# A two-layer decoder trunk in split fp32r: a mean subtracted by VectorE, single PSUM banks in four places, block moves on two queues, one more group by seven products

## The chip, the cores and the metric

The kernel runs on one core of one Trainium2 chip. The metric is the device time of one launch in microseconds, the median of three runs: 2025.73 us for the kernel before (2024.69 to 2026.8). All times below are microseconds unless marked otherwise.

## The reference, cut to what matters

One sequence of 256 tokens, 2048 features, two layers, all in float32. Layer 0 mixes by causal pooling over windows of 2, 4, 8 and 16 tokens, layer 1 by dilated causal attention with 16 heads of 128, whose K and V are computed from the stream behind layer 0. Each mixer and each FFN ends in a residual with DeepNorm and a LayerNorm:

```python
for i in range(DEPTH):
    mix = pool_mixer(h, ...) if i < N_A_LAYERS else dilated_attention(h, k_shared, v_shared, ...)
    h = layer_norm(DEEPNORM_ALPHA * h + mix, ln1_g[i], ln1_b[i])
    u = h @ w_up                      # 2048 -> 2 * 5504
    c = causal depthwise conv of u, width 3, with bias
    gate, val = split(c)
    ff = (silu(gate) * val) @ w_down  # 5504 -> 2048
    h = layer_norm(DEEPNORM_ALPHA * h + ff, ln2_g[i], ln2_b[i])
```

## The kernel before, in words

**Units.** The work is a list of weight units, each a block of 512 rows by up to 512 columns of one matrix. `run_units` takes them in order. For each unit SP loads the raw block (L89), ScalarE rounds it to fp32r as `wh` (L99, a cast), VectorE takes the rest `wl = raw - wh` (L100), and TensorE multiplies both halves with the two halves of the activations, `xc`. Three small products thus stand for one float32 product (L180 and L181, or L183 to L185). Units are loaded and split several units ahead of their use. Work that follows a unit is put off by `later(n, fn)`, which runs `fn` n units on; `before[i]` runs just ahead of unit i. This order of the code is the order of each engine's queue. Tile pools add the waits: a tile that is taken again waits for the last reader of the old one.

**Seven products.** Most blocks of the down projections and of V are multiplied by seven half-size products instead of eight (a form of Strassen's scheme). Such a block is split by `split_sums` into a unit "a" and a unit "b" (L113 and L119 on ScalarE; L114, L120, L121, L122 and L124 on VectorE, which also forms sums of parts of the weights). On TensorE a block by seven has 42 matmuls of 256 columns (L244 to L246), a plain one 24 of 512 (L255 to L257). `sevens[q]` in `ffn` says for which of the four column groups c of the down projection the row quarter q goes by seven. `down(2)` of layer 0 multiplies the quarters 7 and 6; its four column groups are woven between the halves of `up(9)` and `up(10)`.

**LayerNorm by features.** H[0] to H[3] hold the stream as [128, 4, 256] quarters of the features, XC the split copies. `add_last` adds the last projection to H, one column group c at a time. Behind c = 0, `shift` takes an estimate of the mean, and subtracts it from the quarters: H[0] by VectorE (L394) and, in the FFN LayerNorm of layer 0 (`first` false), H[1] to H[3] by three accumulating DMAs on GpSimd's queue (L409). Then each group c adds its products to H[c] (L338, L340), sums and squares are folded into S and Q (L364, L367, L370), and `chain` sums them over partitions on TensorE (L429, L430), from which the norm is built (L434 to L444, L305). Meanwhile TensorE runs a first projection of the unnormalised quarters `xp` (L183 to L185).

**Moves.** Before and after the down projection, the stream is turned between features and tokens: `to_tokens` (all four quarters in both layers) and `to_features` (four column groups in layer 0) transpose 32 by 32 blocks on VectorE (L807, L835) and `moves` carries the blocks across partitions by 16 DMAs per quarter, issued by SP in three parts over three units (L825). `to_tokens` uses one `hb` tile for all quarters of a layer. GpSimd's queue holds the accumulating DMAs of the down projection (L287), half of the moves of the attention (L1101) and the three of L409.

**PSUM.** The pool `psp` has four tiles of two banks. `pair` takes one, `bank` takes one and uses only its first half. A tile's dependences are tracked for the whole pair: at the start `x_quad` writes both halves of a quarter into one pair (L548) and then copies (L553, ScalarE), subtracts (L554, VectorE), copies, subtracts. `outputs` of the attention puts two heads into one pair (L1114, L1115) and evacuates them (L1119, L1120). `finish1` at the very end puts three results into two pairs (L940, L947, L952, L955).

Of the kernel before, what the change touches and what calls it, by code (L numbers as in the profile page):

```python
# [9 lines left out]
F32 = mybir.dt.float32  # L10
# [7 lines left out]
T = 256  # L18
# [14 lines left out]
def trunk(ctx: ExitStack, tc: tile.TileContext, x, pool_w_in, pool_w_grp, pool_scale, pool_w_out,  # L33
# [348 lines left out]
    def shift(s, first, lay, which):  # L382
# [10 lines left out]
        def one():  # L393
            V.tensor_tensor(H[0], H[0], cb, OP.add)  # L394
            if first:
                pre(1)
            stats(0)
# [15 lines left out]
        if not first:  # L413
            for q in (1, 2, 3):
                less(q)
# [120 lines left out]
    def x_quad(q, halves=(0, 1)):  # L536
        xin = XIN
        if halves[0] == 0:
            H[q] = hp.tile([P, 4, T], F32, name="h", tag="h")
            XC[q] = quad_tile("xc")  # L540
        if halves[0] == 0:
            ST["xT"] = pair("xT")
        both = ST["xT"]
        for half in halves:
            for kk in range(2):
                for t in range(2):
                    k = 2 * half + kk
                    PE.transpose(both[:, half, kk * T + t * P:kk * T + t * P + P], xin[q, t][:, k * P:(k + 1) * P],  # L548
                                 ident)
        for half in halves:  # L550
            pv2 = both[:, half, :].rearrange("p (k t) -> p k t", k=2)
            s = slice(2 * half, 2 * half + 2)
            A.copy(XC[q][:, s, 0, :T], pv2)  # L553
            V.tensor_tensor(XC[q][:, s, 1, :T], pv2, XC[q][:, s, 0, :T].bitcast(F32), OP.subtract)  # L554
        if halves[-1] == 1:
            before.setdefault(min(q + 1, 3), []).append(
                lambda: A.copy(H[q], both.rearrange("p b (k t) -> p (b k) t", k=2)))
# [26 lines left out]
    def ffn(lay):  # L584
# [9 lines left out]
        else:  # L594
            sevens[7] = (0, 1)
# [220 lines left out]
    def moves(fr, to):  # L816
# [3 lines left out]
        def part(i, n):  # L820
            if i == 0:
                dst.append(to().rearrange("p (k a j) -> p a k j", k=8, a=4))
            for ab in range(i, i + n):
                a, b = ab // 4, ab % 4
                nc.sync.dma_start(dst[0][32 * b:32 * b + 32, a], fr[32 * a:32 * a + 32, b])  # L825
# [38 lines left out]
    def tm_post(lay, n, c):  # L864
# [68 lines left out]
        def finish1():  # L933
# [4 lines left out]
            ps = [p[:, i, :] for p in (pair("gb"), pair("gb")) for i in range(2)]  # L938
# [166 lines left out]
    def outputs(hq, ms):  # L1105
# [3 lines left out]
        both = pair("o")  # L1109
        for m in ms:  # L1110
            hd = slice(m * P, (m + 1) * P)
            ps = both[:, m % 2, :]
# [3 lines left out]
        o = oq[hq][:, ms[0]:ms[0] + 2]  # L1116
        for at in (slice(0, 1), slice(1, 2)) if hq == 3 else (slice(0, 2),):
            hi = o[:, at, 0, :T]
            A.copy(hi, both[:, at, :T])  # L1119
            V.tensor_tensor(o[:, at, 1, :T], both[:, at, :T], hi.bitcast(F32), OP.subtract)  # L1120
# [157 lines left out]
```

## Time and profile before

| what | value |
|---|---|
| median of 3 runs | 2025.73 us (2024.69 to 2026.8) |
| the profiled execution, its own time | 2024.98 us |
| span of its trace, first to last instruction | 2023.2 us |
| mean granted TensorE clock | 0.999 |
| TensorE matmul (PE) busy | 2011.6 us, 99% |
| VectorE (DVE) busy | 1728.5 us, 85% |
| ScalarE (ACT) busy | 1269.2 us, 63% |
| GpSimd (POOL) busy | 94.3 us, 5% |

The profiled execution's own time is 1.78 us above the span, since it has what lies around the first and the last instruction, and 0.75 us under the median. Rows of the trace have the start in us from the span's start, the duration, the engine, the line and operation, the tiles, how often, and in brackets the idle time ahead of it with what ended it. Matmuls are pipelined, so a row's duration overlaps the next: what a matmul costs is the distance between starts.

### The profile page before, as it was taken

How to read it: one execution, taken by the hardware profiler on the slowest of the kernel's cores; microseconds unless marked ns; L12 is line 12 of the kernel's file. 1: busy time of each engine (PE TensorE's matmuls, PEld its weight loads, DVE VectorE, ACT ScalarE, POOL GpSimd, SP SyncE). 2: the span in 40 equal slices, each digit the busy share in tenths (PEclk: the TensorE clock that was granted, in tenths of full speed). 3: DMA queues.
4: the chain of work that ended last, by engine and by line, in shares of the span. 5: the costliest groups of instructions: out<-in, count | busy, mean ns of one | idle time of the engine just before them, and what ended most of it. 6: DMA issues, size and time to landing. Idle time of an engine off the chain costs nothing.

```text
span 2023.2 us, 31428 instructions
## 1 busy us (share of the span) xinstructions
PE 2011.6 (99%) x12742; PEld 1813.7 (90%) x12742; DVE 1728.5 (85%) x1822; ACT 1269.2 (63%) x1546; POOL 94.3 (5%) x154
## 2 busy tenths in 40 slices
PE   9999999999999999999999999999999999999999
PEld 8898988999899988888898988998899989989987
DVE  6868887999899999779796878787899899989898
ACT  5454686766766676656554444477767677667672
POOL 2000000000000000000000021000000000000000
PEclk9999999999999999999999999999999999999999
DMA  8565576676666767885565656557666757666765
GB/s 256 192 211 188 164 216 191 180 221 222 197 198 205 233 190 219 236 226 187 177 207 165 199 175 207 188 175 221 167 215 203 227 179 227 193 222 189 211 220 173
DMA packets 271825, 408.30 MB, mean 202 GB/s; under 512 B 74446, under 2 KB 86116, under 8 KB 271424
## 3 DMA queue, kind: packets, MB, share of 16 engines
q1 hardware_dynamic: 259488, 388.93, 59.1%
q0 software_dynamic: 11760, 16.70, 5.5%
q8 instruction: 100, 1.64, 0.3%
q10 hardware_dynamic: 432, 0.66, 0.1%
q14 instruction: 45, 0.37, 0.1%
HBM read 380.01 MB, written 2.10 MB: 189 GB/s over the span
## 4 chain that ended last, share of the span: by engine, by line
PE 98%; DVE 1%; DMA 0%; issue 0%; ACT 0%; SPq 0%; DVEq 0%
PE acc L180 44%; PE acc L181 22%; PE s L246 3%; PE s L244 3%; PE s L245 3%; PE acc L185 3%; PE t L246 2%; PE t L244 2%; PE t L245 2%; PE acc L184 2%; PE acc L183 2%; PE t L255 2%; PE t L257 2%; PE t L256 2%; PE s L1064 0%; PE o L1114 0%
## 5 line engine op out<-in xcount | busy, mean ns | idle before, releaser
L180 PE MATMUL acc<-xc,wh 128*128 128x512 f32 x3264 | 1151.8, 396 | 0.0
L181 PE MATMUL acc<-xc,wl 128*128 128x256 f32 x3264 | 916.0, 281 | 0.0
L100 DVE TENSOR_TENSOR wl<-raw,wh 128x2048 fp32r<-128x2048 f32 (+2 forms) x305 | 657.1, 2163 | 174.9 <-ACT wh L99 170.3
L180 PEld LDWEIGHTS acc<-xc,wh 128*128 128x128 f32 x3264 | 616.0, 189 | 143.3
L99 ACT CAST wh<-raw 128x2048 fp32r<-128x2048 f32 (+2 forms) x305 | 548.7, 1805 | 170.1 <-PE acc L180 70.4
L181 PEld LDWEIGHTS acc<-xc,wl 128*128 128x128 f32 x3264 | 615.4, 189 | 0.1
L113 ACT CAST wh<-raw 128x1024 fp32r<-128x1024 f32 x142 | 148.4, 1052 | 194.5 <-DVE raw L122 175.3
L114 DVE TENSOR_TENSOR wl<-raw,wh 128x1024 fp32r<-128x1024 f32 x142 | 169.4, 1221 | 11.2 <-ACT wh L113 11.2
L121 DVE TENSOR_TENSOR wl<-raw,wh 128x1536 fp32r<-128x1536 f32 x71 | 124.5, 1754 | 6.7 <-ACT wh L119 5.7
L119 ACT CAST wh<-raw 128x1536 fp32r<-128x1536 f32 x71 | 104.9, 1477 | 35.4 <-PE acc L180 28.2
L287 POOL DMA_DIRECT2D ht<-w x48 | 41.3, 1014 | 1446.7 <-DVE ht L877 722.1
L246 PE MATMUL t<-wh,g 128*128 128x256 f32 x376 | 105.7, 281 | 0.0
L244 PE MATMUL t<-wh,g 128*128 128x256 f32 x376 | 105.6, 281 | 0.0
L245 PE MATMUL t<-wl,g 128*128 128x256 f32 x376 | 105.4, 280 | 0.0
L620 ACT ACTIVATE c<-u,cv 128x256 f32<-128x256 f32 x172 | 89.5, 592 | 23.1 <-DVE f L682 16.6
L246 PE MATMUL s<-wh,xs 128*128 128x256 f32 x344 | 96.2, 280 | 0.0
L244 PE MATMUL s<-wh,xs 128*128 128x256 f32 x344 | 96.1, 279 | 0.0
L245 PE MATMUL s<-wl,xs 128*128 128x256 f32 x344 | 96.0, 279 | 0.0
L124 DVE TENSOR_TENSOR raw<-raw 128x1024 f32<-128x1024 f32 x71 | 87.0, 1225 | 2.4
L625 ACT ACTIVATE a<-u,cv 128x256 f32<-128x256 f32 x172 | 73.4, 499 | 11.9 <-DVE g L692 11.9
L611 ACT COPY u<-acc 128x512 f32<-128x512 f32 x84 | 46.9, 573 | 47.4 <-PE acc L181 47.1
L625 ACT ACTIVATE u<-u,cv 128x256 f32<-128x256 f32 x172 | 73.4, 499 | 0.0
(337 smaller groups left out, 3445.2 us busy)
## 6 DMA issues: line engine op xcount, KB each, us to landing
raw<-in_ffn_w_up_dram SPq DMA_DIRECT2D x160, 1024.0 KB, 5.2
raw<-in_ffn_w_down_dram SPq DMA_DIRECT2D x80, 1024.0 KB, 5.2
raw<-in_pool_w_out_dram SPq DMA_DIRECT2D x16, 1024.0 KB, 5.0
raw<-in_shared_w_k_dram SPq DMA_DIRECT2D x16, 1024.0 KB, 5.1
raw<-in_attn_w_q_dram SPq DMA_DIRECT2D x16, 1024.0 KB, 5.1
raw<-in_shared_w_v_dram SPq DMA_DIRECT2D x16, 1024.0 KB, 5.2
raw<-in_attn_w_o_dram SPq DMA_DIRECT2D x16, 1024.0 KB, 5.4
ht<-w POOLq DMA_DIRECT2D x50, 256.0 KB, 5.3
```

What stands on the lines that cost most here:

```text
L99: A.copy(wh[i][:, s], r[:, s])
L100: V.tensor_tensor(wl[i][:, s], r[:, s], wh[i][:, s].bitcast(F32), OP.subtract)
L113: A.copy(h[:, :, n], r[:, :, n])
L114: V.tensor_tensor(l[:, :, n], r[:, :, n], h[:, :, n].bitcast(F32), OP.subtract)
L119: A.copy(hs, rs)
L121: V.tensor_tensor(ls, rs, hs.bitcast(F32), OP.subtract)
L180: PE.matmul(ps[m].ap, h[:, k, c], q[:, k, :, :T], start=st, stop=False)
L181: PE.matmul(ps[m][:, :T], l[:, k, c], q[:, k, 0, :T], start=False, stop=sp)
L244: PE.matmul(to, xh, h[:, k, n], start=opens and kk == 0, stop=False)
L245: PE.matmul(to, xh, l[:, k, n], start=False, stop=False)
L246: PE.matmul(to, xl, h[:, k, n], start=False, stop=ends and kk == 1)
L625: A.activation(to[:, m, :], u[:, m, i:i + T], AF.Copy, scale=cv[:, i, j:j + 1])
```

## The change

It has four parts. Lines of the kernel after are given as "after L…".

1. In `shift`, H[1] of layer 0's FFN LayerNorm gets its mean subtracted by VectorE (after L398), right behind H[0]. Only H[2] and H[3] are left to GpSimd's accumulating DMAs.
2. Single PSUM tiles in four places: `x_quad` uses a `bank` for each half, and H is copied in two halves and a unit earlier (after L553); `finish1` uses three banks; `outputs` for the heads 2 and 3 of the last head quarter uses a bank for each head and evacuates each as soon as it is issued; the heads 0 and 1 of that quarter are evacuated together.
3. `moves` issues every second of its 16 DMAs from GpSimd's queue (after L822).
4. `sevens[7]` of layer 0 holds the column group 2 too.

```diff
         def one():
             V.tensor_tensor(H[0], H[0], cb, OP.add)
             if first:
                 pre(1)
+            else:
+                V.tensor_tensor(H[1], H[1], cb, OP.add)
             stats(0)
...
         if not first:
-            for q in (1, 2, 3):
+            for q in (2, 3):
                 less(q)
...
-        if halves[0] == 0:
-            ST["xT"] = pair("xT")
-        both = ST["xT"]
         for half in halves:
+            ps = bank("xT")
             for kk in range(2):
                 for t in range(2):
                     k = 2 * half + kk
-                    PE.transpose(both[:, half, kk * T + t * P:kk * T + t * P + P], xin[q, t][:, k * P:(k + 1) * P],
-                                 ident)
-        for half in halves:
-            pv2 = both[:, half, :].rearrange("p (k t) -> p k t", k=2)
+                    PE.transpose(ps[:, kk * T + t * P:kk * T + t * P + P], xin[q, t][:, k * P:(k + 1) * P], ident)
+            pv2 = ps.rearrange("p (k t) -> p k t", k=2)
             s = slice(2 * half, 2 * half + 2)
             A.copy(XC[q][:, s, 0, :T], pv2)
             V.tensor_tensor(XC[q][:, s, 1, :T], pv2, XC[q][:, s, 0, :T].bitcast(F32), OP.subtract)
-        if halves[-1] == 1:
-            before.setdefault(min(q + 1, 3), []).append(
-                lambda: A.copy(H[q], both.rearrange("p b (k t) -> p (b k) t", k=2)))
+            before.setdefault(q, []).append(lambda s=s, pv2=pv2: A.copy(H[q][:, s, :], pv2))
...
-            sevens[7] = (0, 1)
+            sevens[7] = (0, 1, 2)
...
-                nc.sync.dma_start(dst[0][32 * b:32 * b + 32, a], fr[32 * a:32 * a + 32, b])
+                by = nc.sync if ab % 2 == 0 else nc.gpsimd
+                by.dma_start(dst[0][32 * b:32 * b + 32, a], fr[32 * a:32 * a + 32, b])
...
-            ps = [p[:, i, :] for p in (pair("gb"), pair("gb")) for i in range(2)]
+            ps = [bank("gb") for cc in range(3)]
...
-        both = pair("o")
+        last = hq == 3 and ms[0] == 2
+        both = None if last else pair("o")
         for m in ms:
             hd = slice(m * P, (m + 1) * P)
-            ps = both[:, m % 2, :]
+            ps = bank("o") if last else both[:, m % 2, :]
             t = pT.pop((hq, m))
             PE.matmul(ps[:, :T], vt[:, 0, hd], t[:, :T], start=True, stop=False)
             PE.matmul(ps[:, P:T], vt[:, 1, hd], t[:, T:], start=False, stop=True)
-        o = oq[hq][:, ms[0]:ms[0] + 2]
-        for at in (slice(0, 1), slice(1, 2)) if hq == 3 else (slice(0, 2),):
-            hi = o[:, at, 0, :T]
-            A.copy(hi, both[:, at, :T])
-            V.tensor_tensor(o[:, at, 1, :T], both[:, at, :T], hi.bitcast(F32), OP.subtract)
+            if last:
+                hi = oq[hq][:, m, 0, :T]
+                A.copy(hi, ps[:, :T])
+                V.tensor_tensor(oq[hq][:, m, 1, :T], ps[:, :T], hi.bitcast(F32), OP.subtract)
+        if not last:
+            o = oq[hq][:, ms[0]:ms[0] + 2]
+            A.copy(o[:, :, 0, :T], both[:, :, :T])
+            V.tensor_tensor(o[:, :, 1, :T], both[:, :, :T], o[:, :, 0, :T].bitcast(F32), OP.subtract)
```

VectorE's queue in the FFN LayerNorm of layer 0, from the split ahead of `one` to the first addition of column group 1 (`cs` is the negative mean, `fold` and `sq` are folding space, `acc` the group's PSUM); before:

```order
L100 TENSOR_TENSOR wl_8478<-raw_8392,wh_8477 128x1536
L394 TENSOR_TENSOR h<-h,cs 128x1024
L364 TENSOR_TENSOR fold<-h 128x512
L367 TENSOR_TENSOR S<-fold 128x256
L364 TENSOR_TENSOR fold<-sq 128x512
L367 TENSOR_TENSOR Q<-fold 128x256
L338 TENSOR_TENSOR h<-h,acc 128x512
```

and after:

```order
L100 TENSOR_TENSOR wl_8512<-raw_8427,wh_8511 128x1536
L394 TENSOR_TENSOR h<-h,cs 128x1024
L398 TENSOR_TENSOR h<-h,cs 128x1024
L364 TENSOR_TENSOR fold<-h 128x512
L367 TENSOR_TENSOR S<-fold 128x256
L364 TENSOR_TENSOR fold<-sq 128x512
L367 TENSOR_TENSOR Q<-fold 128x256
L338 TENSOR_TENSOR h<-h,acc 128x512
```

One instruction of 128x1024 comes in between the subtraction of H[0] and the folds; on GpSimd's queue one of the three accumulates goes.

VectorE's queue around the splits of `down(2)`'s column group 2 in layer 0, from the last plain split ahead of it (L849 to L880 and their like are evacuations of the group before, `hb<-ht` is the transpose of `to_features`); before:

```order
L100 TENSOR_TENSOR wl_7557<-raw_7485,wh_7556 128x2048
L100 TENSOR_TENSOR wl_7595<-raw_7514,wh_7594 128x2048
L120 TENSOR_TENSOR raw_7554<-raw_7554 128x2x256
L121 TENSOR_TENSOR wl_7633<-raw_7554,wh_7632 128x2x768
L122 TENSOR_TENSOR raw_7554<-raw_7554 128x2x256
L124 TENSOR_TENSOR raw_7554<-raw_7554 128x4x256
L835 STREAM_TRANSPOSE hb<-ht 128x2x4x128
L114 TENSOR_TENSOR wl_7676<-raw_7554,wh_7675 128x4x256 x2
```

and after:

```order
L100 TENSOR_TENSOR wl_7563<-raw_7493,wh_7562 128x2048
L120 TENSOR_TENSOR raw_7522<-raw_7522 128x2x256
L121 TENSOR_TENSOR wl_7603<-raw_7522,wh_7602 128x2x768
L122 TENSOR_TENSOR raw_7522<-raw_7522 128x2x256
L124 TENSOR_TENSOR raw_7522<-raw_7522 128x4x256
L114 TENSOR_TENSOR wl_7642<-raw_7522,wh_7641 128x4x256 x2
L832 STREAM_TRANSPOSE hb<-ht 128x2x4x128
L120 TENSOR_TENSOR raw_7600<-raw_7600 128x2x256
L121 TENSOR_TENSOR wl_7684<-raw_7600,wh_7683 128x2x768
L122 TENSOR_TENSOR raw_7600<-raw_7600 128x2x256
L124 TENSOR_TENSOR raw_7600<-raw_7600 128x4x256
```

One L100 of 2048 elements has become L120, L121, L122, L124 and two L114; what follows stands a unit later.

ScalarE's queue at the start, from the first quarter of x to the third (`xc<-xT` are the copies out of PSUM, `wh` the casts of the first weights); before:

```order
L553 CAST xc<-xT 128x2x256
L99 CAST wh_173<-raw_93 128x512
L553 CAST xc<-xT 128x2x256
L99 CAST wh_173<-raw_93 128x512 x3
L553 CAST xc<-xT 128x2x256 x2
L99 CAST wh_256<-raw_115 128x512 x4
L557 COPY h<-xT 128x1024
L553 CAST xc<-xT 128x2x256 x2
```

and after:

```order
L551 CAST xc<-xT 128x2x256
L99 CAST wh_173<-raw_93 128x512
L551 CAST xc<-xT 128x2x256
L99 CAST wh_173<-raw_93 128x512 x3
L553 COPY h<-xT 128x512 x2
L551 CAST xc<-xT 128x2x256 x2
L99 CAST wh_260<-raw_115 128x512 x4
L553 COPY h<-xT 128x512 x2
```

The copies of H stand a unit earlier, ahead of the next quarter's casts, and in two halves. On GpSimd's queue there are 96 moves more (after L822), and on SP's 96 fewer: in each part of six or five, SP now has three or two.

## Prediction

> **What bounds the kernel now.** I read the share of busy time first, then which engine TensorE's waits name, then the timelines of the places that the change touches. The engine row, and the waits of TensorE (line waited at, releaser, us in total, times, longest):
>
> ```profile
> PE 2011.6 (99%) x12742; PEld 1813.7 (90%) x12742; DVE 1728.5 (85%) x1822; ACT 1269.2 (63%) x1546; POOL 94.3 (5%) x154
> PE acc L429 <- DVE S L370: 2.6, 1, 2.6
> PE acc L185 <- DVE wl L100: 0.9, 3, 0.3
> PE acc L430 <- DVE Q L370: 0.8, 1, 0.8
> PE acc L180 <- DVE o L1120: 0.5, 2, 0.2
> ```
>
> TensorE is busy for 2011.6 of the span of 2023.2 us. So only two things can shorten the run much: fewer matmul starts, or the few places where TensorE stands. The waits name them: 3.4 us at the sums of one LayerNorm (L429, L430), 0.9 at the start (L185), 0.5 behind the attention's last outputs (L180). VectorE, at 85%, is next, and wherever the change gives it work I ask what has it idle there. I sum against the profiled execution's own time, 2024.98, which is 0.75 under the median of 2025.73.
>
> **A. H[1]'s mean by VectorE.** VectorE around the subtraction, the window up to the sums, then the end of the chain (start, duration, engine, line, tiles, count, idle ahead and its releaser; the window's row has length, then busy us of PE, PEld, DVE, ACT, POOL):
>
> ```profile
> 893.01 1.22 DVE L394 TENSOR_TENSOR h<-h,cs 128x1024 f32<-128x1024 f32 x1
> ...
> 896.32 0.43 DVE L367 TENSOR_TENSOR Q<-fold 128x256 f32<-128x256 f32 x1
> 901.48 0.69 DVE L338 TENSOR_TENSOR h<-h,acc 128x512 f32<-128x512 f32 x1 [4.73 <-DMA h<-cs]
> ...
> 901.48:931.00 29.52, 29.18 (x225) 27.98 (x223) 29.11 (x40) 12.72 (x18) 0.00 (x0) 1.00 0.70 206
> ...
> 932.78 0.43 DVE L370 TENSOR_TENSOR S<-S,fold 128x256 f32<-128x256 f32 x1
> ...
> 934.30 0.43 DVE L370 TENSOR_TENSOR Q<-Q,fold 128x256 f32<-128x256 f32 x1
> ```
>
> VectorE stands 4.73 us for the accumulate into H[1], and from there works 29.11 of 29.52 us up to the sums that TensorE waits for: the stall is carried whole to S and Q. With one more instruction like L394 (1.22) VectorE goes on at 896.75 + 1.25 = 898.0 instead of 901.48, 3.5 earlier. S is then ready at 933.21 − 3.5 = 929.7, Q at 934.73 − 3.5 = 931.2. TensorE there:
>
> ```profile
> 924.73 0.28 PE L183 MATMUL acc<-xp,wh 128*128 128x258 f32 x1
> ...
> 930.38 0.28 PE L185 MATMUL acc<-xp,wl 128*128 128x258 f32 x1
> ...
> 935.45 0.78 PE L183 MATMUL acc<-xp,wh 128*128 128x258 f32 x1
> ...
> 938.31 0.28 PE L183 MATMUL acc<-xp,wh 128*128 128x258 f32 x1
> ```
>
> The last column group's products end where the first row begins, 924.73, and its addition now wanted at 930.28 − 3.5 = 926.8, so these results are no limit. From 924.73 to 930.38 there are 47 steps, 0.120 each. The next projection starts at 935.45. The same place in layer 0's first LayerNorm has no stall:
>
> ```profile
> 224.03 0.28 PE L185 MATMUL acc<-xp,wl 128*128 128x258 f32 x1
> ...
> 224.82 0.47 PE L183 MATMUL acc<-xp,wh 128*128 128x258 f32 x1
> ```
>
> There the sums take 0.79 from start to start, here 5.07: 4.28 lost. Behind the stall the matmuls are slow: 12 steps from 935.45 to 938.31 take 2.86 instead of 1.44, another 1.42. That makes 5.7 in all. Q comes 0.3 late for a chain without a stall (L430 would start at about 930.9), which leaves 5.4. Next behind it stands the split of the normalised quarter:
>
> ```profile
> 951.29 1.22 DVE L305 TENSOR_TENSOR xc<-h,xc 128x1024 fp32r<-128x1024 f32 x1
> ...
> 954.18 0.39 PE L180 MATMUL acc<-xc,wh 128*128 128x512 f32 x1
> ```
>
> It is done at 952.51, 1.67 ahead of its first use. VectorE gains 3.5 and TensorE 5.4, so 1.9 are asked of these 1.67: 0.2 lost, and as much again may be lost at the later quarters. I take **−5.0**, with bounds from −5.7 to −1.5 (where ScalarE's casts, which stand between VectorE's instructions, allow only a part of the 3.5).
>
> **B. Seven products.** TensorE over the plain block, the seven-product block behind it and the next unit; VectorE's instructions of a seven-product split; and two idle stretches of VectorE there:
>
> ```profile
> 807.75 0.40 PE L255 MATMUL t<-wh,g 128*128 128x512 f32 x1
> ...
> 813.32 0.28 PE L244 MATMUL s<-wh,g 128*128 128x256 f32 x1
> ...
> 818.27 0.39 PE L180 MATMUL acc<-xc,wh 128*128 128x512 f32 x1
> ```
>
> ```profile
> 815.08 1.76 DVE L100 TENSOR_TENSOR wl<-raw,wh 128x1536 fp32r<-128x1536 f32 x1 [3.38 <-DMA h<-hb]
> ...
> 828.72 0.68 DVE L120 TENSOR_TENSOR raw<-raw 128x512 f32<-128x512 f32 x1
> ...
> 832.98 1.24 DVE L835 STREAM_TRANSPOSE hb<-ht 128x1024 f32<-128x1024 f32 x1
> 834.14 2.31 DVE L114 TENSOR_TENSOR wl<-raw,wh 128x1024 fp32r<-128x1024 f32 x2
> ```
>
> The plain block takes 5.57, one by seven 4.95: **−0.6**. VectorE pays 4.26 (L120 to L124, from 828.72 to 832.98) + 2.31 (two L114) for one plain split of 2048 elements, about 2.3 by scaling L100's 1.76 for 1536: 4.3 more. Its cover is idle time: VectorE stands 3.38 us right there before L100, and the stretch after has more:
>
> ```profile
> 850.00:882.00 32.00, 32.00 (x184) 27.95 (x183) 21.77 (x19) 17.78 (x19) 1.72 (x2) 1.00 0.84 237
> ```
>
> (10.2 us without work in 32). So I cost it at nothing. If the cover is gone, because the 3.38 is taken by other splits that come due at once, up to 4.3 arrive at TensorE, and a slow stretch like the one above (1.42) with it: bounds −0.6 to +5.1.
>
> **C, D, E. Single banks.** TensorE behind the last outputs; the start (ScalarE, VectorE, TensorE); the tail (TensorE, VectorE):
>
> ```profile
> 1235.15 0.28 PE L181 MATMUL acc<-o,wl 128*128 128x256 f32 x1
> 1235.66 0.50 PE L180 MATMUL acc<-o,wh 128*128 128x512 f32 x1 [0.23 <-DVE o L1120]
> ```
>
> ```profile
> 14.01 0.59 ACT L553 CAST xc<-xT 128x512 fp32r<-128x512 f32 x1 [0.76 <-DVE xc L554]
> ...
> 15.40 0.28 PE L184 MATMUL acc<-xc,wh 128*128 128x256 f32 x1
> 15.97 0.39 PE L185 MATMUL acc<-xc,wl 128*128 128x256 f32 x1 [0.29 <-DVE wl L100]
> ```
>
> ```profile
> 2015.57 2.84 PE L947 MATMUL gb<-g,dg 128*128 128x512 f32 x6
> ...
> 2017.59 1.41 DVE L952 SCALAR_TENSOR_TENSOR ht<-ht,mv,gb 128x512 f32<-128x512 f32 x2 [0.63 <-PE gb L947]
> ```
>
> C: the wait of 0.23 opens a gap of 0.51 from start to start where 0.12 is usual, and the wait row has two such: 2 × 0.39 = 0.8. With a bank per head ScalarE copies each head as its two matmuls end, and no evacuation waits for the other head's: I take **−0.75** (0 to −0.8).
>
> D: ScalarE's second copy waits 0.76 for VectorE to have read the first half of the same pair; with two banks it follows at once, VectorE's splits come some 0.7 earlier, and the gap of 0.57 before L185 goes, 0.45 over the usual. The wait row has three of them, 0.9 us together against this one's 0.29: 0.45 × 0.9 / 0.29 = 1.4. I take **−1.35**. The new copies of H (two, ahead of the next quarter's casts) fall where ScalarE stands for x; a transpose that waits for them as its bank comes free is the loss that I allow: bounds −1.4 to +1.
>
> E: L952 waits for four of the six matmuls, since two results share a pair. With a bank each it starts when VectorE is free, 0.63 earlier; the last two results then set the end: six matmuls are done at 2018.41, against an L955 that starts at 2018.91. I take **−0.45** (0 to −0.5).
>
> **F. Half the moves on GpSimd.** Moves of layer 0's features now (ns min/median/max), the attention's moves on GpSimd (us busy, mean ns), and landings of these from both queues (last column, us):
>
> ```profile
> L825 SPq DMA_DIRECT2D h<-hb x64: 585/609/1582, 773.5 to 877.6; - x64
> ```
>
> ```profile
> L1101 POOL DMA_DIRECT2D pTs<-pb x64 | 36.2, 574 | 297.1 <-issue 155.8 <-DVE f L1001 112.4 <-ACT wh L113 12.7
> ```
>
> ```profile
> pTs<-pb SPq DMA_DIRECT2D x64, 24.0 KB, 3.7
> pTs<-pb POOLq DMA_DIRECT2D x64, 24.0 KB, 3.5
> ```
>
> A move costs SP 609 ns and GpSimd 574, and lands alike. 96 × 0.6 = 58 us leave SP, over stretches in which TensorE never waits for a transfer after the start; GpSimd is idle 95% of the time, and on its queue they pass only the accumulates of L287. VectorE's 3.38 above ends on such a transfer (h<-hb) and would shrink, which only helps B. I take **0**. Bounds from the table of waits: nothing of TensorE's waits is on a move now, so the gain is 0; the loss is the third rival's.
>
> The Trainium skill speaks against this part: "DMA: Bandwidth & Descriptors", section "SWDGE vs HWDGE vs iDMA", says that plain transfers belong on SP or ScalarE, since GpSimd writes descriptors by software into SBUF state that VectorE can lock it out of. By it moves on GpSimd would take longer while VectorE works. The trace does not agree: with VectorE busy 85% overall, 574 ns against 609 and 3.5 us against 3.7.
>
> **Sum.** −5.0 − 0.6 − 0.75 − 1.35 − 0.45 + 0 = −8.15: 2024.98 − 8.15 = 2016.83 for a profiled execution, and 0.75 more at the median's level: 2017.6.
>
> **Rivals.**
>
> 1. *The stall in A is replaced by the next one.* ScalarE's casts or the split at 951.29 come late, and only 2 of A's 5.0 are kept. For it: only 1.67 of slack, and TensorE gains more than VectorE. Against it: VectorE worked without a gap to S. Time 2017.6 + 3 = 2020.6. Still faster.
> 2. *VectorE becomes the bound around the seventh block.* 4.3 of splits arrive late and a slow stretch of 1.4 follows: 2017.6 + 5.7 = 2023.3. For it: VectorE's seven-product splits sit in the densest part. Against it: 3.38 idle there. Counted as no change.
> 3. *GpSimd's moves come late, and it is slower than before.* `to_tokens` has one `hb` for all quarters, so the next quarter's transpose waits for the moves of the one before:
>
> ```profile
> 293.56 3.74 SPq L825 DMA_DIRECT2D ht<-hb  x5
> ```
>
> ```profile
> 302.73 1.24 DVE L807 STREAM_TRANSPOSE hb<-h 128x1024 f32<-128x1024 f32 x1
> ```
>
> The last move is issued by 297.30 and lands some 3.7 later, at 301.0; the transpose comes at 302.73, 1.7 after. If GpSimd's part lands later than that, VectorE stands, with all splits queued behind the transpose, three times in each layer. To be slower by over 0.2% the six must cost 8.15 + 4.1 = 12.2, 2.0 each; at 3 each it is 2017.6 + 18 = 2035.6. Against it: a GpSimd part has two or three moves, so issue ends earlier than SP's five do now.
>
> 4. *The change doesn't do what it says in A:* something other than the accumulate keeps VectorE at 901.48 (the addition waits for TensorE's group 1 or for a tile), and only B to E are left, 2025.73 − 3.15 = 2022.6. Against it: the releaser named is the transfer. Faster by 0.15%, so no change.
>
> **How the numbers follow.** 0.2% of 2025.73 is 4.1 us, about what a measurement of this kernel can tell from no change. My forecast, 2017.6 with its own range of 2016 to 2019.5, has 0.57; rival 1 has 0.21; rival 2 has 0.07; rival 3 has 0.09; rival 4 has 0.06. Faster (forecast and rival 1) 0.78, same (2 and 4) 0.13, slower (3) 0.09. The range from 2015.0 (A at its full 5.7, B's idle shared with F, the noise of a run) to 2023.0 leaves out rivals 3 and most of 2.
>
> **What would show it.** A: no idle before L338 in this LayerNorm, waits at L429 and L430 under 0.5, and steps of 0.12 right behind. B: 42 matmuls (L244 to L246) where L255 to L257 stood, no wait of TensorE from 800 to 840. C, D: the wait rows of L180 on `o` and of L185 on `wl` gone. E: no idle before L952. F: 96 moves of some 0.6 us on GpSimd and no VectorE idle before L807's like. The prediction is wrong if TensorE's wait list holds a new row of over 1 us, above all one on a split (`wl`) or on `xc`.

## The result, and the profile after

The changed kernel took 2016.92 us (median of 5 runs, 2016.64 to 2017.28), the kernel before beside it 2026.22 (5 runs, 2024.69 to 2026.8): a ratio of 0.9957, 95% interval 0.9943 to 0.997. In a second comparison (the tenth experiment) it was 2016.21 against 2024.33, ratio 0.9963, 0.995 to 0.9976. The two profiled executions differ by 8.34 us in their own time (2024.98 and 2016.64) and by 8.3 in span (2023.2 and 2014.9). The forecast was 8.15. The ratios here and below leave out one run of all, in the sixth experiment: it took 2156.99 us at a mean granted clock of 0.851.

The page of the changed kernel and the waits of TensorE (line, releaser, us in total, times, longest):

```profile
PE 2006.7 (100%) x12760; PEld 1811.0 (90%) x12760; DVE 1732.9 (86%) x1827; ACT 1270.3 (63%) x1551; POOL 148.8 (7%) x249
```

```profile
PE acc L183 <- ACT wh L99: 1.8, 1, 1.8
PE warm L1164 <- DVE one L1160: 1.1, 1, 1.1
PE xT L548 <- DMA xin<-in_x_dram: 0.4, 1, 0.4
PE acc L185 <- DVE wl L100: 0.2, 1, 0.2
```

The waits at the LayerNorm's sums and behind the attention's outputs are gone; what is left stands in the first 11 us. To see where the time came from, I set the same matmul of both traces side by side and followed the distance of their starts: after is 1.90 earlier at 32 us (the start), 1.78 ahead of the seventh block, 2.49 behind it, 7.66 behind the LayerNorm's sums and the steps that follow them, 7.36 from 966 on, 8.21 behind the attention's last outputs (places by the trace of before). Each step has its rows.

VectorE in the FFN LayerNorm of layer 0, then TensorE at its sums:

```profile
890.52 1.22 DVE L394 TENSOR_TENSOR h<-h,cs 128x1024 f32<-128x1024 f32 x1
891.65 1.22 DVE L398 TENSOR_TENSOR h<-h,cs 128x1024 f32<-128x1024 f32 x1
...
895.18 0.68 DVE L338 TENSOR_TENSOR h<-h,acc 128x512 f32<-128x512 f32 x1
...
926.65 0.42 DVE L370 TENSOR_TENSOR S<-S,fold 128x256 f32<-128x256 f32 x1
...
928.17 0.42 DVE L370 TENSOR_TENSOR Q<-Q,fold 128x256 f32<-128x256 f32 x1
```

```profile
927.89 0.28 PE L185 MATMUL acc<-xp,wl 128*128 128x258 f32 x1
928.01 0.60 PE L431 MATMUL acc<-S,onesd 128*128 128x256 f32 x2
928.65 0.70 PE L432 MATMUL acc<-Q,onesd 128*128 128x256 f32 x2
929.00 0.47 PE L183 MATMUL acc<-xp,wh 128*128 128x258 f32 x1
...
930.54 0.28 PE L185 MATMUL acc<-xp,wl 128*128 128x258 f32 x1
```

No idle stands ahead of L338 any more. S is ready at 927.07, before its first reader at 928.01; Q at 928.59, just in time. From the last projection to the next it is 1.11 us instead of 5.07, and the steps behind it are short at once. The clock that TensorE was granted tells why they were slow before: 0.50 there, and 1.00 in after (windows behind the sums of before, then of after; the clock is the third number from the end):

```profile
935.00:938.00 3.00, 3.00 (x13) 2.82 (x14) 3.00 (x5) 2.39 (x3) 0.00 (x0) 0.50 0.00 0
930.00:935.00 5.00, 5.00 (x44) 5.00 (x44) 4.42 (x4) 3.42 (x3) 0.00 (x0) 1.00 0.23 68
```

TensorE at the seventh block (start of its third group, start of the block behind, start of the next unit):

```profile
805.97 0.28 PE L244 MATMUL s<-wh,g 128*128 128x256 f32 x1
...
810.83 0.28 PE L244 MATMUL s<-wh,g 128*128 128x256 f32 x1
...
815.78 0.39 PE L180 MATMUL acc<-xc,wh 128*128 128x512 f32 x1
```

The group is through in 4.86, where the plain block took 5.57, and no wait follows it.

TensorE and ScalarE behind the attention's last outputs (ScalarE's first row is of before), and the tail:

```profile
1227.91 0.40 PE L180 MATMUL acc<-o,wh 128*128 128x512 f32 x1
1228.15 0.28 PE L181 MATMUL acc<-o,wl 128*128 128x256 f32 x1
1228.30 0.50 PE L180 MATMUL acc<-o,wh 128*128 128x512 f32 x1
```

```profile
1235.64 0.37 ACT L1119 CAST o<-o 128x256 fp32r<-128x256 f32 x1 [0.49 <-DVE o L1120]
...
1226.76 0.37 ACT L1116 CAST o<-o 128x256 fp32r<-128x256 f32 x1 [3.67 <-PE o L1113]
1227.41 0.37 ACT L1116 CAST o<-o 128x256 fp32r<-128x256 f32 x1 [0.28 <-PE o L1113]
```

```profile
2007.36 2.84 PE L944 MATMUL gb<-g,dg 128*128 128x512 f32 x6
```

```profile
2008.66 1.46 DVE L949 SCALAR_TENSOR_TENSOR ht<-ht,mv,gb 128x512 f32<-128x512 f32 x2
2010.24 0.87 DVE L952 SCALAR_TENSOR_TENSOR ht<-ht,mv,gb 128x256 f32<-128x256 f32 x2
```

ScalarE's second copy now waits for its matmul and not for VectorE, and the two gaps of 0.5 are down to 0.11 and 0.15: TensorE gains 0.85 over the outputs. In the tail VectorE's last row starts 2.88 behind the first L944, where it was 3.34 behind L947: 0.46 gained. The span has little of it, because it ended 3.4 us behind VectorE's last instruction before and 3.7 after.

The moves of layer 0's features, on both queues (ns min/median/max), then their landings in after and, last, in before:

```profile
L822 SPq DMA_DIRECT2D h<-hb x32: 585/608/904, 771.7 to 870.9; - x32
L822 POOL DMA_DIRECT2D h<-hb x32: 582/582/641, 772.0 to 861.5; - x32
```

```profile
h<-hb SPq DMA_DIRECT2D x32, 32.0 KB, 5.7
h<-hb POOLq DMA_DIRECT2D x32, 32.0 KB, 5.1
h<-hb SPq DMA_DIRECT2D x64, 32.0 KB, 3.7
```

GpSimd issues a move in 582 ns, SP in 608. Within the change GpSimd's land sooner (last column, us), but both land later than the 3.7 that SP's took before, when they were alone. No wait of VectorE or TensorE ends on one.

### The profile page after: what moved, and what is told of

Its sections match the earlier page's. It is cut to its first block, busy times and chain, and to the rows that moved or that the text cites. A ratio compares the mean times of both kernels' runs of the same rounds, so it can differ in the third digit from the quotient of the medians.

```text
span 2014.9 us, 31541 instructions
## 1 busy us (share of the span) xinstructions
PE 2006.7 (100%) x12760; PEld 1811.0 (90%) x12760; DVE 1732.9 (86%) x1827; ACT 1270.3 (63%) x1551; POOL 148.8 (7%) x249
## 4 chain that ended last, share of the span: by engine, by line
PE 99%; DVE 1%; DMA 0%; SPq 0%; issue 0%; ACT 0%; DVEq 0%
PE acc L180 44%; PE acc L181 22%; PE s L246 3%; PE s L244 3%; PE s L245 3%; PE acc L184 3%; PE acc L185 3%; PE acc L183 3%; PE t L246 3%; PE t L244 3%; PE t L245 3%; PE t L255 2%; PE t L256 2%; PE t L257 2%; PE s L1061 0%; PE o L1112 0%
## 5 line engine op out<-in xcount | busy, mean ns | idle before, releaser
L180 PE MATMUL acc<-xc,wh 128*128 128x512 f32 x3264 | 1152.1, 396 | 0.0
L100 DVE TENSOR_TENSOR wl<-raw,wh 128x2048 fp32r<-128x2048 f32 (+2 forms) x304 | 655.0, 2162 | 170.2 <-ACT wh L99 167.6
L180 PEld LDWEIGHTS acc<-xc,wh 128*128 128x128 f32 x3264 | 616.0, 189 | 143.5 <-issue 0.3
L114 DVE TENSOR_TENSOR wl<-raw,wh 128x1024 fp32r<-128x1024 f32 x144 | 171.8, 1221 | 11.3 <-ACT wh L113 11.3
L121 DVE TENSOR_TENSOR wl<-raw,wh 128x1536 fp32r<-128x1536 f32 x72 | 126.2, 1752 | 6.6 <-ACT wh L119 5.5
L124 DVE TENSOR_TENSOR raw<-raw 128x1024 f32<-128x1024 f32 x72 | 88.2, 1225 | 2.5
L621 ACT ACTIVATE a<-u,cv 128x256 f32<-128x256 f32 x172 | 73.4, 499 | 11.9 <-DVE g L688 11.9
```

The lines of the kernel that those rows point to most:

```text
L100: V.tensor_tensor(wl[i][:, s], r[:, s], wh[i][:, s].bitcast(F32), OP.subtract)
L114: V.tensor_tensor(l[:, :, n], r[:, :, n], h[:, :, n].bitcast(F32), OP.subtract)
L121: V.tensor_tensor(ls, rs, hs.bitcast(F32), OP.subtract)
L180: PE.matmul(ps[m].ap, h[:, k, c], q[:, k, :, :T], start=st, stop=False)
L621: A.activation(to[:, m, :], u[:, m, i:i + T], AF.Copy, scale=cv[:, i, j:j + 1])
```

## The experiments

My theory going in was that the terms are separate and of the sizes forecast. The rivals were that the mean's part needs the relief of SP's queue, and that the moves are a gain or a loss of their own. "LayerNorm" below is the FFN one of layer 0. In it I measured in each trace the gap from the last projection ahead of the sums to the first behind them, and the 24 steps that follow.

### 1. The mean alone (e1_mean_only)

```diff
             if first:
                 pre(1)
+            else:
+                V.tensor_tensor(H[1], H[1], cb, OP.add)
...
-            for q in (1, 2, 3):
+            for q in (2, 3):
```

> The kernel before with the first part of the change alone: H[1]'s mean by VectorE. The trace of after against before shows TensorE 5.1 us earlier over this LayerNorm and 0.16 lost behind it. Theory of separate terms: 5.0 us faster than before, ratio 0.9975, and the sums (L429, L430) without a wait. Rival, the part needs the others (SP relieved of moves, so that casts and raw weights come earlier): 1.5 to 3 us faster, with a wait left at the sums or a wait of VectorE on a cast in this window.

Measured: 2020.5 against 2023.27, ratio 0.9983 (0.9974 to 0.9992). Against the profiled execution of before TensorE gains 5.14 over the LayerNorm and gives 0.32 back behind it: the gap is 1.14, and no wait is left at the sums or at VectorE's addition:

```profile
898.00 0.68 DVE L338 TENSOR_TENSOR h<-h,acc 128x512 f32<-128x512 f32 x1
```

So the part needs no other. But the medians differ by only 2.8, and the ratio says 3.4 with an interval from 1.6 to 5.3. And the runs of this kernel lie within 0.82 us (11 runs, 2019.87 to 2020.69), those of before within 4.6 (21 runs, 2021.57 to 2026.18). That set the question for the rest: the stall that this part removes is not the same in each execution.

### 2. All but the mean (e2_all_but_mean)

```diff
-            else:
-                V.tensor_tensor(H[1], H[1], cb, OP.add)
...
-            for q in (2, 3):
+            for q in (1, 2, 3):
```

> The changed kernel with H[1] given back to GpSimd's accumulating transfer. Theory of separate terms: the stall is back whole, some 4.7 us of VectorE at L338 on the transfer, 2.6 + 0.8 of TensorE at the sums, a slow stretch behind them, and 4.3 us faster than before where the whole change is 9.3 faster by its medians. Rival, the moves on GpSimd changed the transfer's landing (its queue is busier, or the memory is): VectorE's stall here is under 3 us or over 6, and the difference to the whole change is as much smaller or larger than 5.

Measured: 2017.33 (2016.33 to 2019.21), ratio 0.9966 (0.9954 to 0.9979), only some 0.4 to 1.1 over the changed kernel. VectorE's wait, and TensorE's:

```profile
897.93 0.69 DVE L338 TENSOR_TENSOR h<-h,acc 128x512 f32<-128x512 f32 x1 [1.95 <-DMA h<-cs]
```

```profile
PE acc L430 <- DVE Q L370: 0.8, 1, 0.8
```

The expectation of a whole stall fell: 1.95 instead of 4.73, no wait at S, 0.8 at Q, and the 24 steps behind are quick (3.09). The rival's mark (under 3) is met here; whether the moves are the reason is for experiments 4, 8 and 9.

### 3. Two quarters by VectorE (e3_two_quarters)

```diff
                 V.tensor_tensor(H[1], H[1], cb, OP.add)
+                V.tensor_tensor(H[2], H[2], cb, OP.add)
...
-            for q in (2, 3):
+            for q in (3,):
```

> The changed kernel with H[2]'s mean by VectorE too, and only H[3] left to GpSimd. It puts 1.25 us more of VectorE ahead of the sums. In the trace of after S is ready at 927.07 and first used at 928.01, Q at 928.60 and used at 928.65. Theory that VectorE's chain sets the sums, with no room left at Q: Q comes 1.25 later, TensorE loses 1.2 at L430 and some 0.3 to 1.4 in slow steps behind it: 1.2 to 2.6 us slower than the changed kernel, about 7 faster than before. Rival, the chain has room elsewhere (VectorE waits for casts or for TensorE's results in between): no difference to the changed kernel.

Measured: 2017.13 (2016.21 to 2018.7), which can't be told from the changed kernel by the times; the trace can:

```profile
929.06 0.70 PE L433 MATMUL acc<-Q,onesd 128*128 128x256 f32 x2 [0.82 <-DVE Q L370]
```

One more instruction (L338 now starts 1.13 later behind the shift) makes TensorE wait 0.82 at Q and the gap 2.07 instead of 1.11, 0.96 of loss. No slow steps follow (24 in 3.08), so it is a little less than I expected. VectorE's chain sets the sums, and the changed kernel has no room left in it.

### 4. Half the moves on GpSimd alone (e4_moves_only)

```diff
-                nc.sync.dma_start(dst[0][32 * b:32 * b + 32, a], fr[32 * a:32 * a + 32, b])
+                by = nc.sync if ab % 2 == 0 else nc.gpsimd
+                by.dma_start(dst[0][32 * b:32 * b + 32, a], fr[32 * a:32 * a + 32, b])
```

> The kernel before with every second move on GpSimd's queue and nothing else. Theory: no wait of TensorE is on a move, so ratio 1.000 within 0.0005, TensorE's starts shifted by under 0.3 us anywhere, and VectorE's 3.4 us idle on a move (h<-hb) gone. Rival, moves on GpSimd help by relieving SP: 0.5 to 1.5 us faster, which would make up what the medians have over the spans (9.3 against 8.3). Rival, they hurt through the one hb tile: a wait of VectorE at the transposes L804 and over 1 us slower.

Measured: 2024.08 against 2023.27, ratio 1.0002 (0.9993 to 1.0011): no difference, as the theory has it. No transpose waits. But two marks of my expectation failed. VectorE's 3.38 of idle time is still there, at the same distance from TensorE as before, and now the trace names ScalarE's cast for it:

```profile
816.94 1.76 DVE L100 TENSOR_TENSOR wl<-raw,wh 128x1536 fp32r<-128x1536 f32 x1 [3.38 <-ACT wh L99]
```

In e1, which has all moves on SP, the same row has 3.38 and names the cast too, and in before the cast ends at 815.05, just ahead of the split at 815.08. So the cast sets this idle time, and my reading of it as a wait for a move (h<-hb) was wrong. And TensorE's starts shift by more than 0.3: they are 1.8 late by 16 us, behind the first weights, and lose 1.1 more at one transfer of the attention, a row that no other trace here has:

```profile
1235.14 0.67 PE L1115 MATMUL o<-pTs,vt 128*128 128x256 f32 x2 [0.83 <-DMA pTs<-pb]
```

Neither place is at a move that the edit touches. The LayerNorm's stall is there:

```profile
902.42 0.69 DVE L338 TENSOR_TENSOR h<-h,acc 128x512 f32<-128x512 f32 x1 [3.82 <-DMA h<-cs]
```

So the moves alone don't make the accumulate land early, and the rival of experiment 2 isn't the whole of it.

### 5. The start alone (e5_start_only)

```diff
-            ST["xT"] = pair("xT")
-        both = ST["xT"]
         for half in halves:
+            ps = bank("xT")
...
+            before.setdefault(q, []).append(lambda s=s, pv2=pv2: A.copy(H[q][:, s, :], pv2))
```

> The kernel before with x_quad's single banks and the earlier copies of H, nothing else. In the trace of after TensorE is 1.9 us earlier by 32.1 us, although a wait of 1.8 on a cast of the first weights (its raw block landed 1.2 later than in the trace of before) cost 0.4 at 12.0. Theory that banks take away the chain copy, subtract, copy, subtract, and all splits behind it come earlier: 1.9 us faster than before; and if the late block is chance, the first transposes of the second quarter stand at 11.6 to 12.0 again either way, since x lands there. Rival, only the three gaps of the first 31 us go: 1.35 faster, and gaps remain at 30.6 to 32.

Measured: ratio 0.9989 (0.9981 to 0.9998), 2.2 us, where the medians differ by 1.0. In the trace TensorE is 0.71 later than before at the second quarter's transposes (the first weights landed late again) and 1.62 earlier at 32.1 us: 2.33 gained between. The changed kernel gains 2.26 there (0.36 late, 1.90 early). By the trace the theory held, and 1.35 was too little. The edit holds both the banks and the earlier copies of H; which of them brings how much was not told apart. Being without the mean's part, this trace has the LayerNorm's stall:

```profile
898.28 0.69 DVE L338 TENSOR_TENSOR h<-h,acc 128x512 f32<-128x512 f32 x1 [3.14 <-DMA h<-cs]
```

### 6. Outputs and tail alone (e6_outputs_and_tail)

```diff
-            ps = [p[:, i, :] for p in (pair("gb"), pair("gb")) for i in range(2)]
+            ps = [bank("gb") for cc in range(3)]
...
-            ps = both[:, m % 2, :]
+            ps = bank("o") if last else both[:, m % 2, :]
```

> The kernel before with single banks in outputs (heads 2 and 3 of the last quarter) and in finish1. Theory: TensorE gains 0.75 at L180 on o, and VectorE another 0.45 at the end, but the last store then lands later from its issue, as in after (span end 3.8 us behind VectorE's last instruction against 3.4): 0.75 to 1.2 faster, ratio 0.9994 to 0.9996, hard to tell from none by the times alone; the trace's starts tell it. Rival, the tail's end is set by a queue of stores and not by VectorE: VectorE ends 0.45 earlier against TensorE, the span by nothing of it.

Measured: ratio 0.9988 (0.9979 to 0.9997), 2.4 us with an interval from 0.6 to 4.2; the medians differ by 1.1. In the trace TensorE gains 0.86 at L180 behind the outputs, VectorE 0.46 more in the tail, 1.3 together, and the span ends 3.2 us behind VectorE. From VectorE's last instruction to the end it was 3.2 to 3.8 in the traces with the banks and 3.3 to 3.9 in those without, so what the changed kernel's profiled execution gave back there (0.32) lies within chance. Its stall at L338 was 1.96, and TensorE had no wait at S.

### 7. Seven products alone (e7_seventh_only)

```diff
-            sevens[7] = (0, 1)
+            sevens[7] = (0, 1, 2)
```

> The kernel before with quarter 7's third column group by seven products and nothing else. Theory: 0.6 us faster (5.57 against 4.95), VectorE's extra 4.3 us covered by its idle time, no wait of TensorE. Rival, the cover came from the moves on GpSimd, which took VectorE's wait of 3.4 on h<-hb away: here VectorE is late, a wait of TensorE on wl of over 0.5 us appears between 800 and 830, and the kernel is 0 to 5 us slower.

Measured: 2023.83 against 2023.64, ratio 0.9999 (0.999 to 1.0008): nothing. TensorE gains 0.72 and loses 1.5 some 75 us further on:

```profile
892.31 0.36 PE L384 MATMUL shift<-S,ones 128*128 128x256 f32 x1 [1.26 <-DVE S L367]
```

Neither theory had that place. VectorE's debt isn't paid by then: a split ahead of the mean, and the cast that it waits for, come late because their raw block does:

```profile
867.88 2.29 DVE L100 TENSOR_TENSOR wl<-raw,wh 128x2048 fp32r<-128x2048 f32 x1 [2.33 <-ACT wh L99]
```

```profile
865.94 1.91 ACT L99 CAST wh<-raw 128x2048 fp32r<-128x2048 f32 x1 [3.87 <-DMA raw<-in_ffn_w_down_dram]
```

The same split in before:

```profile
863.95 2.29 DVE L100 TENSOR_TENSOR wl<-raw,wh 128x2048 fp32r<-128x2048 f32 x1 [2.27 <-ACT wh L99]
```

TensorE is 1.66 later here than there, the split 3.93: it has lost 2.3 against TensorE, about half of the 4.3.

### 8. All moves on GpSimd (e8_all_moves_on_gpsimd)

```diff
-                nc.sync.dma_start(dst[0][32 * b:32 * b + 32, a], fr[32 * a:32 * a + 32, b])
+                by = nc.gpsimd
+                by.dma_start(dst[0][32 * b:32 * b + 32, a], fr[32 * a:32 * a + 32, b])
```

> The kernel before with all 16 moves of a quarter on GpSimd's queue, twice the dose of the change. Theory that issue and landing are as quick there as on SP (0.58 us each): no difference, ratio 1.000 within 0.0005, no wait of VectorE at the transposes. Rival of the prediction that comes out slower: moves land late, VectorE stands at the transposes of to_tokens for the one hb tile, six times; over 1 us slower. A weaker rival: the accumulates of the down projection (L287) stand behind moves on GpSimd's queue, and a wait on ht appears.

Measured: ratio 0.9996 (0.9987 to 1.0004): twice the dose, no difference. No transpose waits. The third rival of the prediction is refuted at both doses. With all moves on one queue they land as they did from SP alone:

```profile
h<-hb POOLq DMA_DIRECT2D x64, 32.0 KB, 3.7
```

So the 5.1 and 5.7 of the changed kernel go with the use of both queues at once, not with GpSimd's. The stall at L338 was 3.29.

### 9. Seven products with the moves (e9_seventh_and_moves)

```diff
-            sevens[7] = (0, 1)
+            sevens[7] = (0, 1, 2)
...
+                by = nc.sync if ab % 2 == 0 else nc.gpsimd
```

> The kernel before with the seventh block's third group by seven products and half the moves on GpSimd. Alone, the seven products saved 0.6 us of TensorE and gave 1.4 back at the mean of the FFN LayerNorm (shift waited 1.3 for VectorE); there raw blocks of w_down were issued behind moves on SP's queue. Theory that half the moves off SP is the cover that the seven products need: TensorE keeps its 0.6 from 815 to the LayerNorm, no wait at the shift. Rival, the wait at the shift comes from VectorE's 4.3 us of added work itself: it is here again, 1 us or more.

Measured: 2020.54 against 2024.33, ratio 0.9985 (0.9976 to 0.9994). No wait at the shift: TensorE keeps its 0.72. The split that was late in experiment 7:

```profile
861.66 2.29 DVE L100 TENSOR_TENSOR wl<-raw,wh 128x2048 fp32r<-128x2048 f32 x1 [2.20 <-ACT wh L99]
```

It stands 2.3 earlier than in before, with TensorE 0.1 earlier: 2.2 of lead instead of 2.3 of debt. With the moves alone (experiment 4) the lead is 2.2 too, with the seven products or without. The other traces with both parts (after, e2, e3, e10) have no wait at the shift either, and e7, with the moves left on SP, has 1.26. So the room for the third group comes from taking half the moves off SP's queue. The rest of the gain of some 3 us is in the LayerNorm:

```profile
898.67 0.69 DVE L338 TENSOR_TENSOR h<-h,acc 128x512 f32<-128x512 f32 x1 [2.04 <-DMA h<-cs]
```

Its 11 runs lie within 1.8 us (2019.81 to 2021.59).

### 10. The change again (e10_change_again)

The changed kernel as it is, with no edit.

> The changed kernel once more, against before on the chip of this call. In the other calls before's medians were 2023.3 and 2023.6, not 2026.2, and its VectorE stall on the accumulate was 1.9 to 4.7 us by chance of the transfer's landing. Theory that the first profiled execution of before had the long end of this stall, so that the mean's part is worth some 3.0 to 3.5 on average and not 5.0: the change is 6 to 7.5 us faster here, at 2016 to 2017.5, and its runs spread over less than half of before's. Rival, the 9.3 of the first comparison is the effect: 8.5 to 9.5 faster.

Measured: 2016.21 (2015.98 to 2016.52) against 2024.33 (21 runs, 2021.11 to 2026.7), ratio 0.9963 (0.995 to 0.9976): 8.1 by medians, 7.5 by the ratio. It lies between my two expectations. Its 5 runs spread over 0.5 us, before's 21 over 5.6.

### 11 and 12. More groups by seven (e11_eight_groups, e12_and_layer_1)

```diff
-            sevens[7] = (0, 1, 2)
+            sevens[7] = every
```

> The changed kernel with quarter 7's fourth column group by seven products too. Theory that VectorE still has cover behind 850 (14.3 busy of 20): 0.6 us faster than the changed kernel in TensorE's starts, no wait. Rival, VectorE's 4.3 more land just ahead of the FFN LayerNorm, whose sums have under 0.1 us of room at Q: 1 to 4 us slower than the changed kernel, with a wait at shift or at the sums.

```diff
-            sevens[9] = (0, 2)
+            sevens[9] = (0, 1, 2)
```

> The kernel of the run before, and in layer 1 quarter 9's second column group by seven products as well. Theory: another 0.6 faster in TensorE's starts (1.2 under the changed kernel), since layer 1 has no moves back to features. Rival, VectorE is at its limit in the last down projection: waits on wl appear near the end, up to 4 us slower.

Measured: 2016.52 (2015.9 to 2019.15), ratio 0.9969 (0.9957 to 0.9981), not faster than the changed kernel; and 2022.99, ratio 0.9995 (0.9986 to 1.0004), 6.8 slower than it. The second edit stands on top of the first. In the first, TensorE gains 0.68 at 840 and gives 0.67 back at the shift:

```profile
886.88 0.35 PE L384 MATMUL shift<-S,ones 128*128 128x256 f32 x1 [0.43 <-DVE S L367]
```

In the second, with layer 1's group too, a split is late in the last down projection:

```profile
1987.75 0.79 PE L256 MATMUL t<-wl,g 128*128 128x512 f32 x1 [2.34 <-DVE wl L100]
```

and TensorE runs slow behind it, at a granted clock of 0.50:

```profile
1987.50:1990.50 3.00, 2.75 (x7) 2.17 (x8) 2.52 (x3) 2.06 (x2) 0.00 (x0) 0.50 0.56 191
```

It was 9.0 earlier than before at 1978.6 and is 2.7 earlier at the last matmuls, where it waits another 1.5 for VectorE (L942). VectorE is late in both, as the rivals have it, though in the first it costs only what the group gains. The third group is the last that brings anything here; no kernel tried beats the changed one.

### What the stall in the LayerNorm costs

In every trace with the transfer, the negative mean, VectorE's subtraction and the end of Q's first fold stand at nearly the same distance behind the shift (0.32 to 0.40, 3.78 to 3.87 and 7.51 to 7.59 us). Only the landing of the accumulate differs (all in us):

```
kernel       VectorE waits at L338   gap over the sums   24 steps behind
before       4.73                    5.06                4.32
e4           3.82                    3.83                4.58
e8           3.29                    3.30                4.57
e5           3.14                    3.45                4.28
e7           2.08                    2.09                3.09
e9           2.04                    2.05                3.08
e6           1.96                    1.97                3.09
e2           1.95                    1.96                3.09
after, e1    none                    1.11, 1.14          3.10
```

Gap and steps together are 4.21 in the changed kernel, 5.05 to 5.18 with a stall of 2 us, 7.7 to 8.4 with 3.1 to 3.8, and 9.38 in the profiled execution of before. So the part is worth 0.9 us or 3.5 to 5.2, by when the transfer lands, and there is a jump between, because the slow steps appear. They are a matter of the clock: in before, e4, e8 and e5 TensorE's granted clock is 0.50 for one stretch of 3.4 us right behind the sums, and in the other traces it stays at 1.00 there. That before's runs scatter over 4.6 to 5.6 us, and those of after, e1 and e10 over 0.5 to 0.8, fits it. So does the mean clock of each run: of before's 75 runs in experiments 1 to 12, the 24 with a mean clock of 1.0 took 2021.1 to 2024.6, the 17 with 0.998 took 2025.2 to 2026.7. One stretch of 3.4 us at half the clock takes 0.0008 off the mean, so the 24 had none; how many the others had, and where, is not on record. The other kernels without this transfer, e3 and e11, scatter over 2.5 and 3.3. They have small waits of their own at Q and at the shift, and whether these grow in the longer runs no trace shows.

What stays open is why the transfer lands early or late. In the two traces whose first accumulate lands latest (12.2 us behind the shift in before; 11.9 in e1, where VectorE doesn't wait for it) the weight load ahead of it landed 2.5 to 2.7 behind the shift, and the next one about 8. In six of the seven other traces with the transfer the one landed 0.4 to 0.5 ahead of the shift, and the other 6.0 to 6.6 behind it. So the latest landings go with late weight loads. But within those six the transfer still lands at 9.4 (e2, e6, e9) or at 10.6 to 11.2 (e4, e5, e8). Moves alone, at either dose, don't make it early (e4, e8), and the loads on SP's queue around it stand at the same distances in e4 (stall 3.82) and e9 (2.04). e9's narrow runs hint that both parts together make it land early more often; one trace of each kernel can't show it, and it wasn't tried further.

## Why the prediction was right, point by point

The sum came out: 8.15 forecast, 8.34 between the profiled executions, 9.3 and 8.1 by medians. The mechanisms of A, C, D and E are the forecast ones. That the sum is so close is partly luck: D brought 0.4 more than forecast and C 0.1 more, A 0.1 less, and the span's end took 0.3 back by chance. And A was sized on an execution with a long stall, to which the result was then compared; against the average of before's later runs the change is worth 7.5 by the ratio. By its steps:

- **A, the mean, −5.0:** −5.17 over the LayerNorm and 0.30 lost behind it (three splits of normalised quarters, 0.1 each), −4.87 in these two traces. The working held: Q's lateness (0.3), slow steps, and VectorE's start, which came 3.8 earlier instead of 3.5. But the term was sized by one execution, and that one had the longest stall of all eight traces that hold this transfer. On average it is worth less: 3.4 by the ratio of experiment 1, 0.9 where the transfer lands early. So the mechanism stands, and its size on average does not.
- **B, seven products, −0.6:** −0.71, as the working had it; but the cover that I named, VectorE's idle time, is too small by itself. Alone the part gains nothing: half of the 4.3 is still owed at the shift, where TensorE waits 1.26. I said of the moves that they only help B; they are what keeps B's gain, and not in the way I said. They don't shorten VectorE's 3.38, which ends on a cast. With half of them off SP's queue the weight load behind the late split lands 2.2 earlier against TensorE, and the split with it (e4, e9).
- **C, outputs, −0.75:** −0.85 in the trace of after, −0.86 alone. The row behind the first gap was slow too (0.33 from start to start against 0.23), which I hadn't counted.
- **D, the start, −1.35:** −1.9 at 32 us (−1.78 from 100 on), 2.3 counted from the second quarter's transposes; both are beyond my bound of −1.4. The three gaps that I scaled are gone and brought 1.7 with the step behind each. So are three more, worth 0.25, 0.25 and 0.08, that I hadn't counted, since no wait row names them. TensorE before:

```profile
30.63 0.28 PE L184 MATMUL acc<-xc,wh 128*128 128x256 f32 x1
30.88 0.39 PE L185 MATMUL acc<-xc,wl 128*128 128x256 f32 x1
...
31.23 0.28 PE L184 MATMUL acc<-xc,wh 128*128 128x256 f32 x1
31.48 0.39 PE L185 MATMUL acc<-xc,wl 128*128 128x256 f32 x1
```

  L185 starts 0.25 behind L184 where 0.12 is usual: VectorE's splits of a quarter (four in 2.43 there) come slower than TensorE uses them, one gap a piece.
- **E, the tail, −0.45:** −0.46 at VectorE's last instruction. The span then ended 0.32 later behind it, which other traces show with no such change.
- **F, moves, 0:** no difference at one dose and at two. The Trainium skill's rule that plain transfers belong on SP or ScalarE ("DMA: Bandwidth & Descriptors", section "SWDGE vs HWDGE vs iDMA") finds no support here: 582 ns against 608 to issue, and 3.7 us to land from either queue alone (before, e8). What I had wrong is that the moves' landings stay as they are: on two queues at once they took 5.1 and 5.7, which cost nothing.

Of the rivals, the first (a backlog takes A's place) showed 0.3 of its 3; the second (VectorE late after the seventh block) happened, but at the shift, at 1.5 instead of 5.7, and only without the moves or with one group more.

One sign that I had named for a wrong prediction did show: a new wait row of over 1 us, TensorE's 1.8 at 9.87 us for the cast of the first weights. It is not the change's. The kernel before has such a row with the mean alone (e1, 1.8) and with the moves alone (e4, 1.6), the second run of the changed kernel (e10) has none, and it costs 0.4 at 12 us.

## What to carry to other kernels

A stall that ends on a transfer should be sized from several executions: here a landing that varied by 3 us made a term vary by 4, since TensorE's clock fell behind the longer stands, and what removing it bought first is a narrow spread. Parts that look separate may share a queue: an edit that costs TensorE nothing may need another edit's room on the loads' queue. And where a wait list shows one gap per block, look at the starts behind it for smaller gaps that no wait row names.

## What the runs showed of the hardware

- TensorE's steps behind the sums fall into two kinds: 24 in 3.08 to 3.10 us where the gap over the sums was up to 2.09, and 4.28 to 4.58 where it was 3.30 or more. In the second kind the granted clock was 0.50 for one stretch of 3.4 us (934.8 to 938.2 in before), in the first it stayed at 1.00. The gaps hold the two sums, so TensorE's recorded waits were at most 0.8 us in the first kind and 1.8 to 3.4 in the second. "TensorE: Matmul & The Clock Gate" of the Trainium skill speaks of idle windows of about 3.4 us; here 1.8 in two pieces with sums between them had the effect (e5: 1.0 and 0.8). A wait's length alone doesn't decide: waits of 1.6 to 2.0 near 10 us are followed by a half clock in e2, e4 and e7, and waits of 1.7 to 2.1 there aren't in after, e1, e5 and e11.
- The first weights' second piece lets ScalarE begin its cast at anything from 7.97 to 9.70 us in the fourteen traces: up to 1.7 us of chance in the first 12.
- Three accumulating transfers of 512 KB on GpSimd's queue took 12.1 to 13.5 us (median of the three) to land in the different traces, two 9.6 to 12.1, one 8.0. The first of the three, the one that VectorE waits for, took 8.4 to 11.2.
- Moves of 32 KB landed 3.7 to 3.9 us behind their issue with all on SP's queue (before, e5, e7) or all on GpSimd's (e8), and 5.0 to 5.7 with half on each (after, e4, e9; layer 0's features, medians).
